# A mixture of experts cut into 28 blocks per layer instead of 31

## The chip, the cores and the metric

The kernel runs on one NeuronCore of a Trainium2 chip. The metric is device time in microseconds (us) for one execution. The engines are PE (TensorE, matrix products; PEld is its weight load), DVE (VectorE), ACT (ScalarE), POOL (GpSimd) and SP (SyncE, which issues the DMAs of the weight stream).

## What is computed

A network of 256 tokens of width 1024: two layers with a mixer (a gated MLP, then block attention) and a mixture of experts, followed by two layers of feed-forward, pooling and recurrence. The change touches the two mixtures of experts. Cut to what matters:

```python
scores = jax.nn.sigmoid(xt @ w_router)            # 256 tokens, 64 experts
choice = where(emask, scores + e_bias, NEG_INF)    # 4 of 8 groups of experts stay
_, eidx = lax.top_k(choice, 8)                     # 8 experts for each token
w = take(scores, eidx); w = w / w.sum(-1) * 2.5
routed = sum over the 8 of w * ((silu(x @ wg[e]) * (x @ wu[e])) @ wd[e])   # width 1024 -> 256 -> 1024
shared = swiglu(xt, ws_gate, ws_up, ws_down)       # one expert for all tokens
return routed + shared
```

All of it is fp32. An expert's three matrices are 3 MB. There are 256 x 8 = 2048 pairs of token and expert, 32 for an expert on average, and the number for each is known only when the router has run.

## The kernel before

All weights come through one stream: SP issues DMAs of 1024 KB, in an order fixed when the program is built, into `ring`, nine slots of 1024 KB. The DMA for a slot waits until the products that read the slot before are done. `pump` issues as far ahead as the ring allows. One slot is one third of an expert: gate and up for the first half of the input features, the same for the second half, and down.

In a mixture of experts (`moe`) the experts are ranked by the number of their tokens, on the chip. The routed experts are computed in blocks of 128 token places each. A block of kind H holds one expert with up to 128 tokens, M two experts with up to 64 each, L four with up to 32 each. `HCAP, MCAP, LCAP` (line 25) give the number of blocks of each kind; the ranks are handed out in that order, so the H blocks take the experts with the most tokens. `blocks_of_ranks` spreads the kinds evenly over the order of work. Tokens beyond a capacity are counted in `route5`, and `overflow` (L1208 to L1237) computes them in a loop over all 64 experts, one at a time, only when there are any.

The order of work on PE is written out by hand, one step for each block b:

- `gu(b, 0)` and `gu(b, 1)`: the gate and up products (L285, read as `ring` and `farena`, output 512 wide), each half needing one slot for each expert of the block; between them `htr(b - 1)`, two transposes (L1156);
- `dn(b - 1)`: the down products of the block before (`ring` and `tmp`), one slot for each expert;
- `pre(b + 1)`: a few small products for the weights and the scatter matrix of the next block (L1120);
- `gather`: half of the gather of the tokens of the next pair of blocks, 16 products of `rarena` with `WH` and `WL` (the tokens);
- `scat(b - 1)`: 16 products that put the block's output back in token order, and four sums on DVE (L1204).

For each expert of a block, `gu` and `dn` use their own columns of the PE array: 128 for H, 64 for each of two in M, 32 for each of four in L, so that the block's experts are side by side in the array. Each `gu` half streams as many slots as there are experts. `htr` of a block needs its activation on ACT and DVE, so it is put behind the first half of the next block's `gu`. In the first five steps the shared expert's products stand among these, and two half slots of its weights (`shd`) in the stream.

Of the kernel before, what the change touches and what calls it, by code (L numbers as in the profile page):

```python
# [24 lines left out]
HCAP, MCAP, LCAP = 12, 12, 7  # L25
# [47 lines left out]
class Item:  # L73
    # slots of the weight stream with whether they are split, matrix products, stages of what follows them,
    # the ring slots that these may take, which buffers of split weights the item still uses otherwise,
    # and how many stages come before the next split
# [7 lines left out]
class Split:  # L84
# [3 lines left out]
    def __call__(self, c, n):  # L88
        # columns c .. c + n of the slot
        b, o = divmod(c, 1024)  # L90
        return self.hi[b][:, o:o + n], self.lo[b][:, o:o + n]
# [3 lines left out]
def moba_moe_hybrid_kernel(ctx: ExitStack, tc: tile.TileContext, A: dict):  # L95
# [14 lines left out]
    x = sb([128, KD, T], F32, "x")  # L110
# [32 lines left out]
    def rview(off, n):  # L143
        # operands in float32r
        assert off + n <= RW, (off, n)
        return rarena[:, off:off + n]
# [11 lines left out]
    # ---------------------------------------------------------------- weight stream  # L158
# [9 lines left out]
    def spare(slot, n, off=0):  # L168
        # fp32 scratch in slots that the stream leaves alone
        v = ring[:, slot:].rearrange("p s f -> p (s f)")  # L170
        return v[:, off:off + n]
# [21 lines left out]
    def ring_slots(*slots):  # L193
        # from here on the stream uses these slots; the others are scratch until it gets them back
        def hold():
            st["held"] = set(range(NRING)) - set(slots)
        add(hold, nsplit=0)
        st["nring"] = slots
# [8 lines left out]
    def run():  # L207
# [14 lines left out]
        def split_halves(idx):  # L222
            # the halves of the next slot to split, if its buffers are free
            q = stt["next"]
            if q >= len(order) or q >= stt["used"] + 2:
                return
            j = order[q]
            n = items[j].first
            if any(idx < i < j and q % 2 in items[i].fence for i in fences) or n >= st["issued"]:
                return  # L230
            stt["next"] += 1
            w = items[j].slots[0][0][2]
            parts = []
            for c in range(0, w, 1024):
                m = min(1024, w - c)
                b = (q % 2) * 2 + c // 1024
                parts.append((WH[:, b, :m], WL[:, b, :m], slot_ap(n)[:, c:c + m]))
            handles[j] = Split([p[0] for p in parts], [p[1] for p in parts])
            for hi, lo, raw in parts:
                S.copy(hi, raw)  # L240
            yield
            for i, (hi, lo, raw) in enumerate(parts):
                V.tensor_sub(lo, raw, hi)  # L243
                if i == len(parts) - 1:
                    donef[n] = True
                    pump()
                yield
# [35 lines left out]
    # ---------------------------------------------------------------- small pieces  # L283
# [31 lines left out]
    def rsqrt_cols(v, y, a, n=2):  # L315
        # v: fp32 columns; y: result
        V.tensor_scalar(a.bitcast(I32), v.bitcast(I32), 1, None, op0=ALU.logical_shift_right)
        V.tensor_scalar(y.bitcast(I32), a.bitcast(I32), -1, 0x5F3759DF, op0=ALU.mult, op1=ALU.add)
        for _ in range(3):
            V.tensor_mul(a, y, y)  # L320
            V.scalar_tensor_tensor(a, a, -0.5, v, op0=ALU.mult, op1=ALU.mult)
            V.scalar_tensor_tensor(y, a, 1.5, y, op0=ALU.add, op1=ALU.mult)
# [3 lines left out]
    def sq_buf():  # L326
        # eight chunks of squares
        return [t[:, i * T:(i + 1) * T] for t in [tmp512() for _ in range(4)] for i in range(2)]
# [4 lines left out]
    def stat_mm(sqs, b=STB):  # L333
        # sums of four chunks at a time, on the four column groups
# [4 lines left out]
    def stat_sum(between=None):  # L339
        # sum over the groups (and 32 equal rows of each) to one column per half of the tokens  # L340
# [23 lines left out]
    def mod_h(Ac, Bc, H, L, ks=range(KD)):  # L364
        # H + L = x * A * R + B, per feature chunk
# [20 lines left out]
    def proj_a(w, p, H, L):  # L386
        # token-major: 256 columns
# [5 lines left out]
    def down_d(w, hid, first, last):  # L393
        # hid: two (H, L) chunks; accumulates all 8 output chunks in banks 0..3
# [17 lines left out]
    # ---------------------------------------------------------------- constants  # L412
# [17 lines left out]
    def lru_consts():  # L430
        # 4 * softplus(-lam); pool bias times pool scale
# [6 lines left out]
        # log1p(e) = 2 atanh(e / (2 + e))  # L438
# [18 lines left out]
    # ---------------------------------------------------------------- ada vectors  # L457
    GB = 6

    def gemv_items(g, out, bname, boff, bank=GB):  # L460
        # eight weight slots; out: [128, 16] columns
# [21 lines left out]
    def gemv_half(h, out, bname, boff, bank=GB):  # L483
        # half as many columns, two rows of the slots at a time; out: [128, 8] columns
# [24 lines left out]
    def interleave(main, side, per):  # L509
        # spread side items among main ones, `per` main items to one side item  # L510
# [28 lines left out]
    # ---------------------------------------------------------------- gMLP (layer 0)  # L539
# [5 lines left out]
    def gmlp():  # L545
# [67 lines left out]
        for s in range(8):  # L613
# [11 lines left out]
            def post2(s=s):  # L625
                # a quarter of the normalised v
# [7 lines left out]
        def spatial(j):  # L634
            # chunks 2 j and 2 j + 1, of group j
# [64 lines left out]
    # ---------------------------------------------------------------- routing: what needs no token, and scores  # L700
# [5 lines left out]
    def route_prep(l):  # L706
        # router rows times the modulation's scale, and what its shift contributes
# [15 lines left out]
    # The weights of the shared expert's first hidden chunk wait where the sum of outputs will be, those of the second wait split.  # L723
# [11 lines left out]
    def shared_second(l):  # L735
        # an item that splits the second hidden chunk's
# [23 lines left out]
    # ---------------------------------------------------------------- swiglu with split weights  # L760
# [10 lines left out]
    def raw_start(lst):  # L771
        # the first three of a list of (arguments of up_pe, post stages, slots): they work on h without the norm's row
        # factor, which comes about meanwhile; their posts follow the third
# [8 lines left out]
    def swiglu_items(uname, u0, dname, d0, nch, hidH, hidL, evac, fin, nh, opts=None, lag=0):  # L782
        # hidden chunks pairwise; evac(p, H, L) of a chunk; fin after the last down slot
# [57 lines left out]
    # ---------------------------------------------------------------- mixture of experts  # L841
# [4 lines left out]
    def moe(l, tail):  # L846
        # the buffers of split weights that come free first hold the tokens, the others the outputs
        # and the weights of the shared expert
# [47 lines left out]
        # ---- norm, router logits  # L896
        def route1():
# [10 lines left out]
            for i in range(4):  # L908
                # token-major copies of x, times the norm's row factor
# [27 lines left out]
        def route1b():  # L937
            p = PB[RB]
            # counts (replicated rows and a column), exact in bfloat16
# [7 lines left out]
            # ranks by descending count  # L947
# [10 lines left out]
        def route2():  # L958
            # positions, weights, order of capacities
# [12 lines left out]
            # into the order of ranks  # L972
# [13 lines left out]
            # for route5  # L986
# [10 lines left out]
        def route5():  # L997
            # capacities by expert, and what goes beyond them
# [19 lines left out]
        # ---- the shared expert, by halves of weight slots among the blocks  # L1018
        sgate = view(6400, T)

        def shw(j):
            if j in (2, 3):
                return SHU1[j - 2]
            # the first output comes later than the second half
# [37 lines left out]
        # ---- blocks of slots  # L1062
# [99 lines left out]
        def dn(b):  # L1162
# [15 lines left out]
            # with the last block the buffers of the tokens become those of split weights again, with scat_last the rest  # L1178
# [111 lines left out]
    # ---------------------------------------------------------------- attention (layer 1)  # L1290
    def attention():
# [9 lines left out]
        # outputs take the place of h  # L1301
# [27 lines left out]
        def kq(nm, s, H, L):  # L1329
# [15 lines left out]
            def hq():  # L1345
                # h of the queries, by pieces
# [14 lines left out]
        def scores(s):  # L1361
            # heads pairwise, masked, softmax over the keys of the upper and the lower half of the queries
# [31 lines left out]
        def weights():  # L1394
            # divide by the sums
# [57 lines left out]
    def att_start(upd):  # L1453
        # residual sums and squares; what the norms of layer 1 scale by
# [13 lines left out]
    # ---------------------------------------------------------------- block 2  # L1468
# [3 lines left out]
    def transition(upd, gname, goff):  # L1472
        # residual sum, the next h (without the norm's row factor) and squares, chunk by chunk
# [14 lines left out]
    # The second block's input is rmsnorm(x) * fin = x R1 fin, whose own norm has the row factor  # L1488
    # R2 = rsqrt(R1^2 mean((x fin)^2) + eps): its first product works on x fin gain, and R1 R2 follows.
# [84 lines left out]
    def hybrid(l, fin):  # L1574
# [131 lines left out]
        def lru_heads(*cs):  # L1706
            # 1 - a^2 = tanh(z / 2) (1 + a)^2 where a = exp(-z)
# [90 lines left out]
        # output chunk m of w_lru_up is complete after unit 10 m + 9  # L1798
# [15 lines left out]
def pack(inp):  # L1814
# [23 lines left out]
    up = lambda w, m: w.reshape(8, 128, -1, m, 128).transpose(2, 1, 3, 0, 4).reshape(-1, 128, 2048)      # (k p) (s m c)  # L1838
    down = lambda w: w.reshape(-1, 2, 128, 1024).transpose(0, 2, 1, 3).reshape(-1, 128, 2048)             # (s kk p) n
    vproj = lambda w: w.reshape(8, 128, -1, 256).transpose(2, 1, 0, 3).reshape(-1, 128, 2048)             # (k p) (s c)  # L1840
    gated = lambda w: w.reshape(8, 128, 2, -1, 128).transpose(3, 1, 2, 0, 4).reshape(-1, 128, 2048)       # (k p) ab (j c)
# [57 lines left out]
```

## Time and profile before

| | |
|---|---|
| median of 3 runs | 2657.63 us (2657.23 to 2666.97) |
| span of the profiled execution | 2661.0 us (its page gives no other time for it) |
| PE busy | 2536.1 us (95%) |
| ACT, DVE busy | 1069.4 us (40%), 1390.8 us (52%) |
| DMA of expert weights | 384 transfers of 1024 KB |
| mean DMA rate over the span | 272 GB/s |
| first expert DMA of layer 0, of layer 1 | 234.4 us, 947.5 us after the start |
| first matmul of the last down product, layer 0, layer 1 | 782.6 us, 1497.6 us |

Matmuls overlap in the array, so a busy PE is not PE at its peak: the order and the starts of its instructions say more than their durations. The rate of the DMAs in a stretch, in GB/s, tells how near the stream is to what it can move; the share of time in which PE waits for it stands in the timeline.

### The profile page before, as it was taken

Reading aid. Unit: us, or ns where it says so; the run is one execution under the profiler, and the core shown is the slowest. Engines: PE = TensorE matmul, PEld = TensorE weight load, DVE = VectorE, ACT = ScalarE, POOL = GpSimd, SP = SyncE. Lnnn points to the kernel's source line nnn. Section 1 sums busy time; section 2 is a strip of 40 time slices with the busy share of each in tenths; the row PEclk is TensorE's granted clock in tenths of the full one; section 3 lists DMA queues with packets and bytes.
Section 4 is the critical chain, followed back from the end, with each engine's and each line's share of the span. In section 5 each row is a group of like instructions: output and inputs, shape, how many; then the busy total and the mean of one; then the engine's idle time right before and its main releaser. Section 6 shows DMA issues by size and latency. Waiting matters only on the chain. (4 is left out here: it accounts for less than half of the span.)

```text
span 2661.0 us, 44584 instructions
## 1 busy us (share of the span) xinstructions
PE 2536.1 (95%) x18198; PEld 1971.5 (74%) x18198; DVE 1390.8 (52%) x2598; ACT 1069.4 (40%) x1766; POOL 3.8 (0%) x6
## 2 busy tenths in 40 slices
PE   6998999999989979999999899999999999999998
PEld 4885554555447845545554599999999999999998
DVE  4555233333347643323333465688655655887655
ACT  3433222222225532222222344576544544685543
POOL 0000000000000000000000000000000000000000
PEclk8999999999999989999999999999999999999999
DMA  9878899999976469999999745354655554454750
GB/s 377 317 269 333 330 374 402 396 404 384 380 293 259 178 279 354 358 422 378 399 404 382 274 167 188 124 188 175 244 183 189 176 189 159 152 178 163 264 188 17
DMA packets 101442, 724.51 MB, mean 272 GB/s; under 512 B 11248, under 2 KB 12528, under 8 KB 14192
## 3 DMA queue, kind: packets, MB, share of 16 engines
q1 hardware_dynamic: 100080, 718.32, 69.1%
q8 instruction: 146, 2.39, 0.4%
q10 hardware_dynamic: 1152, 3.28, 0.3%
q14 instruction: 64, 0.52, 0.1%
HBM read 720.50 MB, written 1.05 MB: 271 GB/s over the span
## 5 line engine op out<-in xcount | busy, mean ns | idle before, releaser
L285 PE MATMUL pb<-rarena,WH 128*128 128x256 f32 x3664 | 722.6, 284 | 36.4 <-DVE farena L1204 23.8
L240 ACT CAST WH<-ring 128x1024 fp32r<-128x1024 f32 x476 | 489.5, 1047 | 454.4 <-PE pb L285 372.5
L285 PE MATMUL pb<-hH,WH 128*128 128x256 f32 x2336 | 665.3, 285 | 3.3 <-ACT hH L1502 2.4
L285 PE MATMUL pb<-hH,WL 128*128 128x256 f32 x2336 | 662.2, 283 | 1.4 <-DVE WL L243 1.4
L285 PE MATMUL pb<-hL,WH 128*128 128x256 f32 x2336 | 661.8, 283 | 0.0
L243 DVE TENSOR_TENSOR WL<-ring,WH 128x1024 fp32r<-128x1024 f32 x476 | 570.9, 1216 | 146.6 <-ACT WH L240 132.8
L285 PEld LDWEIGHTS pb<-rarena,WH 128*128 128x128 f32 x3664 | 598.4, 190 | 54.6 <-ACT farena L1107 33.3
L285 PE MATMUL pb<-rarena,WL 128*128 128x256 f32 x2336 | 616.5, 280 | 3.6 <-DVE WL L243 2.3
L285 PE MATMUL pb<-ring,farena 128*32 128x512 f32 (+2 forms) x2064 | 464.9, 598 | 7.8 <-DMA ring<-ex 7.8
L285 PEld LDWEIGHTS pb<-hH,WH 128*128 128x128 f32 x2336 | 448.9, 192 | 15.6 <-ACT WH L240 5.0
L285 PEld LDWEIGHTS pb<-hH,WL 128*128 128x128 f32 x2336 | 448.8, 192 | 2.0 <-DVE WL L243 1.9
L285 PEld LDWEIGHTS pb<-hL,WH 128*128 128x128 f32 x2336 | 449.0, 192 | 0.2 <-DVE hL L1499 0.2
L285 PEld LDWEIGHTS pb<-rarena,WL 128*128 128x128 f32 x2336 | 444.2, 190 | 5.0 <-DVE WL L243 3.0
L285 PEld LDWEIGHTS pb<-ring,farena 128*32 128x32 f32 (+2 forms) x2064 | 150.8, 135 | 231.2 <-issue 207.5
L285 PE MATMUL pb<-ring,tmp 128*32 128x512 f32 (+2 forms) x1024 | 246.4, 608 | 14.7 <-PEq L1216 5.8
L1144 DVE SCALAR_TENSOR_TENSOR tmp<-pb,small,tmp 128x256 f32<-128x256 f32 x62 | 30.0, 484 | 423.4 <-ACT tmp L1142 423.4
L285 PEld LDWEIGHTS pb<-ring,tmp 128*32 128x32 f32 (+2 forms) x1024 | 78.8, 136 | 176.7 <-issue 157.4
L1177 DVE TENSOR_TENSOR WL<-pb,WH 128x512 fp32r<-128x512 f32 x124 | 85.8, 692 | 193.0 <-ACT WH L1176 193.0
L1204 DVE TENSOR_TENSOR farena<-farena,pb 128x512 f32<-128x512 f32 x232 | 149.1, 684 | 70.6 <-PE pb L285 70.6
L828 DVE TENSOR_TENSOR tmp<-pb,R 128x512 f32<-128x512 f32 x88 | 60.8, 691 | 203.0 <-PE pb L285 199.0
L1107 ACT ACTIVATE farena<-pb,adac,Acol 128x256 f32<-128x256 f32 x256 | 124.9, 561 | 72.0 <-PE pb L285 71.7
L1176 ACT CAST WH<-pb 128x512 fp32r<-128x512 f32 x124 | 72.8, 587 | 199.3 <-PE pb L285 199.3
(302 smaller groups left out, 1644.9 us busy)
## 6 DMA issues: line engine op xcount, KB each, us to landing
ring<-ex SPq DMA_DIRECT2D x384, 1024.0 KB, 12.0
ring<-ada SPq DMA_DIRECT2D x56, 1024.0 KB, 8.1
ring<-f1u SPq DMA_DIRECT2D x44, 1024.0 KB, 4.9
ring<-f2u SPq DMA_DIRECT2D x44, 1024.0 KB, 5.0
ring<-win SPq DMA_DIRECT2D x40, 1024.0 KB, 4.8
ring<-f1d SPq DMA_DIRECT2D x22, 1024.0 KB, 4.8
ring<-f2d SPq DMA_DIRECT2D x22, 1024.0 KB, 4.8
ring<-lu SPq DMA_DIRECT2D x10, 1024.0 KB, 4.7
```

The source lines that it names most:

```text
L240: S.copy(hi, raw)
L243: V.tensor_sub(lo, raw, hi)
L285: P.matmul(out, l, r, start=start, stop=stop, skip_group_check=True, **kw)
L828: V.tensor_tensor(t.rearrange("p (a t) -> p a t", a=2), hold["p"].rearrange("p (a t) -> p a t", a=2), R.rearrange("p (o t) -> p o t", o=1) ...
L1107: S.activation(xg[:, pi % 2, k], bank[:, i * T:(i + 1) * T], AF.Identity, scale=Acol[:, 2, k:k + 1], bias=sh2(l)[:, k:k + 1])
L1144: V.scalar_tensor_tensor(hh, bank[:, 256:], wsl[:, b % 2:b % 2 + 1], t[:, :256], op0=ALU.mult, op1=ALU.mult)
L1176: S.copy(yH[:, fs], PB[DN[f]])
L1177: V.tensor_tensor(yL[:, fs], PB[DN[f]], yH[:, fs], op=ALU.subtract)
L1204: V.tensor_tensor(a2, a2, bank, op=ALU.add)
```

## The change

The counts of blocks of each kind change: two H and three M fewer, two L more. The 64 experts stay (10 + 2 x 9 + 4 x 9, before 12 + 2 x 12 + 4 x 7), and so do the 192 transfers of their weights in each layer, in the same order of use within a block. The capacities by rank become 128 for the first 10, 64 for the next 18 and 32 for the last 36 (before: 12, 24, 28).

```diff
-HCAP, MCAP, LCAP = 12, 12, 7
+HCAP, MCAP, LCAP = 10, 9, 9
```

The rest of the diff only takes out comments. The order of the kinds that `blocks_of_ranks` makes, before and then now:

```
LHMLHMHMLHMLHMHMLHMHMLHMHMLHMHM
LHMLHMLHMLHMLHMLHMLHMLHMLHMH
```

On PE in layer 0, the step of block 6 (`pb_63` and `pb_64` are the PSUM banks of gate and up, `pb_65` and `pb_66` those of down, `farena` the gathered tokens, `tmp` the hidden values, `rarena` with `WH` and `WL` a scatter):

```order
 L285 MATMUL pb_68<-rarena,WH 128x256
 L285 MATMUL pb_68<-rarena,WL 128x256
-L285 MATMUL pb_63<-ring,farena 128x512 x4
+L285 MATMUL pb_63<-ring,farena 32x512 x16
 L1156 MATMUL pb_64<-cst,tmp 128x128 x2
-L285 MATMUL pb_63<-ring,farena 128x512 x4
+L285 MATMUL pb_63<-ring,farena 32x512 x16
 L285 MATMUL pb_65<-ring,tmp 64x512 x2
```

Where an H block stood, with one slot of weights in each half, there is an L block, with four in each half.

On PE at the end of layer 0, the last step with a `gu`; before:

```order
L285 MATMUL pb_63<-ring,farena 64x512 x8
L1156 MATMUL pb_64<-cst,tmp 128x128 x2
L285 MATMUL pb_63<-ring,farena 64x512 x8
L285 MATMUL pb_65<-ring,tmp 128x512
L285 MATMUL pb_66<-ring,tmp 128x512
```

and now:

```order
L285 MATMUL pb_64<-ring,farena 128x512 x4
L1156 MATMUL pb_63<-cst,tmp 128x128 x2
L285 MATMUL pb_64<-ring,farena 128x512 x4
L285 MATMUL pb_65<-ring,tmp 64x512 x2
L285 MATMUL pb_66<-ring,tmp 64x512 x2
```

The last block is an H after an M, where it was an M after an H. Since 28 is even, the last pair of blocks is whole; with 31 it held one block and a half of zeros, and its gather was as long as the others. The instructions of the other stages are the same.

## Rows read from the trace of the kernel before

**Rows 1.** The page: its first line, and the busy time of each engine.
```profile
span 2661.0 us, 44584 instructions
PE 2536.1 (95%) x18198; PEld 1971.5 (74%) x18198; DVE 1390.8 (52%) x2598; ACT 1069.4 (40%) x1766; POOL 3.8 (0%) x6
```

**Rows 2.** Stretches of both expert stages; last columns: granted PE clock, DMA share, GB/s.
```profile
370.00:410.00 40.00, 39.20 (x222) 19.60 (x221) 13.43 (x33) 8.16 (x17) 0.00 (x0) 1.00 0.83 313
410.00:510.00 100.00, 95.45 (x515) 49.18 (x512) 32.21 (x71) 23.22 (x48) 0.00 (x0) 1.00 1.01 420
330.00:750.00 420.00, 405.98 (x2244) 214.38 (x2243) 142.09 (x313) 99.92 (x205) 0.00 (x0) 1.00 0.96 392
1040.00:1460.00 420.00, 407.56 (x2252) 214.44 (x2248) 141.49 (x312) 101.12 (x207) 0.00 (x0) 1.00 0.96 392
```

**Rows 3.** DMAs of expert weights: issues, time to landing, SP's waits for PE.
```profile
ring<-ex SPq DMA_DIRECT2D x384, 1024.0 KB, 12.0
...
DMA to landing us min/median/max: 4.6/12.0/20.1
...
SPq L1074 <- PE pb L285: 518.5, 157, 10.0
```

**Rows 4.** PE timeline, layer 0, 592 to 655: start, busy us, products with weights.
```profile
592.87 3.65 PE L285 MATMUL pb<-ring,tmp 128*64 128x512 f32 x16
...
601.45 3.65 PE L285 MATMUL pb<-ring,farena 128*64 128x512 f32 x16
...
608.99 3.70 PE L285 MATMUL pb<-ring,tmp 128*128 128x512 f32 x8
612.12 0.68 PE L285 MATMUL pb<-rarena 128*128 128x8 f32 x2
...
617.50 3.64 PE L285 MATMUL pb<-ring,farena 128*32 128x512 f32 x32
...
625.01 4.57 PE L285 MATMUL pb<-ring,tmp 128*64 128x512 f32 x16
629.51 0.38 PE L285 MATMUL pb<-rarena 128*128 128x2 f32 x2
...
634.50 3.60 PE L285 MATMUL pb<-ring,farena 128*128 128x512 f32 x8
...
641.68 4.19 PE L285 MATMUL pb<-ring,tmp 128*32 128x512 f32 x32
...
650.88 3.65 PE L285 MATMUL pb<-ring,farena 128*64 128x512 f32 x16
```

**Rows 5.** PE timeline, layer 0: products in which PE waited for weights.
```profile
410.27 4.67 PE L285 MATMUL pb<-ring,tmp 128*64 128x512 f32 x16
...
456.17 1.05 PE L285 MATMUL pb<-ring,farena 128*32 128x512 f32 x4
...
459.98 3.62 PE L285 MATMUL pb<-ring,farena 128*32 128x512 f32 x26 [1.44 <-DMA ring<-ex]
463.53 1.07 PE L285 MATMUL pb<-ring,tmp 128*64 128x512 f32 x2
...
468.54 0.38 PE L285 MATMUL pb<-rarena 128*128 128x2 f32 x2
...
544.40 4.58 PE L285 MATMUL pb<-ring,tmp 128*64 128x512 f32 x16
...
706.24 1.07 PE L285 MATMUL pb<-ring,tmp 128*64 128x512 f32 x2
708.66 3.65 PE L285 MATMUL pb<-ring,tmp 128*64 128x512 f32 x14 [1.35 <-DMA ring<-ex]
```

**Rows 6.** Stretches of 2 us in and after a wait of PE; columns as in rows 2.
```profile
458.00:460.00 2.00, 0.56 (x5) 0.02 (x3) 0.00 (x0) 0.00 (x0) 0.00 (x0) 1.00 1.00 418
782.00:784.00 2.00, 1.35 (x4) 0.59 (x6) 1.44 (x4) 0.00 (x0) 0.00 (x0) 0.50 0.05 8
```

**Rows 7.** PE timeline, end of layer 0: the last down product.
```profile
782.64 6.18 PE L285 MATMUL pb<-ring,tmp 128*64 128x512 f32 x16 [3.26 <-DVE x L1243]
```

## The prediction

> **What bounds the kernel now.** I read the page first: PE is busy for 95% of the span [rows 1]. That is a share of busy time over stages with different limits, so it says only where to look. Next I cut the two expert stages into stretches [rows 2]. In 410 to 510 the stream moves 420 GB/s for 100 us without a break, and in 370 to 410 only 313. Over 420 us of either layer the mean is 392. So the stream runs at its limit in some places and is held up in others, and who holds it up stands in SP's waits: 518.5 us for PE's products to free a slot [rows 3]. The two limits alternate, PE in the stretches with few experts per block and the stream where the blocks of four stand close together. A change that takes work from one of them is therefore worth at most what the other leaves.
>
> Then I read a cycle of blocks in PE's timeline [rows 4]. A block's gate and up products run from 601.45 to 608.99 for an M (7.54 us), from 617.50 to 625.01 for an L (7.51) and from 634.50 to 641.68 for an H (7.18). The reader is to see that these hardly differ: four experts side by side in the array take as long as one, although they read four times the weights. The down product is 3.13 us for an H (608.99 to 612.12). For an M it is 4.50 (625.01 to 629.51), of which 4.57 - 3.65 = 0.92 is a wait for weights (the same product lasts 3.65 at 592.87), so 3.58 in itself; I take the same for an L. PE's time goes by blocks, the stream's by experts, and the change trades the one against the other: fewer blocks, the same 192 transfers.
>
> **What the change saves on PE.** A step from one block's start to the next is 16.05 us (601.45 to 617.50), 17.00 - 0.92 = 16.08 (617.50 to 634.50) and 16.38 - (4.19 - 3.65) = 15.84 (634.50 to 650.88), without waits. Taking the products above from each leaves 5.38, 4.99 and 5.08 us for the rest of a step (small products, gather, scatter), 5.15 in the mean. A block thus costs 7.18 + 3.13 + 5.15 = 15.5 us as H, 16.3 as M, 16.2 as L. The change removes two H and three M and adds two L: 2 x 15.5 + 3 x 16.3 - 2 x 16.2 = 47.5 us for a layer. One more half gather goes, because 31 blocks need as many gathers as 32: about 2 us (5.15 less the small products is two runs of 16 products, 2.2 each at most). Together 49.5 us for a layer, 99 for both, if nothing else ended last. DVE and ACT lose the same steps; they are half busy [rows 1], so their share is counted at nothing. The cover is PE itself, which they follow in each step; without it the four DVE sums of a scatter would be next.
>
> **What the stream gives back.** A transfer is 1024 KB, 1.0486 MB; at 420 GB/s it takes 2.50 us. Seven experts, one L, one H and one M, are 21 transfers or 52.4 us. PE needs 16.05 + 16.08 + 15.84 = 48.0 us for these three blocks. The new order is nine such triples and a last H, so PE must wait 52.4 - 48.0 = 4.4 us in each triple once the ring's stock is used up. Before, the order had HM between the triples more often, and there the stream could catch up.
>
> When is the stock used up? The kernel before shows it. The first six blocks have the same kinds as now. Before, the next L came after LHMHM, and its following down product waited 4.67 - 3.65 = 1.02 us (at 410). The L after that came only three blocks later, and it paid in full: from 456.17 to 468.54 is 12.37 us for half a gate product and a down product that need 3.6 + 3.58, a wait of 5.2 us [rows 5]. That is the new order's steady state, seen once, and near the 4.4 of the sum. So I count one wait of 1.0 us at the third L and 4.4 at each of the six after it: 27.4 us. The waits that stood there before go: 1.02, 5.2, 0.93 (at 544), 0.92 and 3.65 + 708.66 - 706.24 - 3.65 = 2.42 (at 706), 10.5 us. Net 16.9 us a layer, and the gain is 49.5 - 16.9 = 32.6.
>
> The stream alone gives a second way to the same number. In 330 to 750 it could have moved its bytes in 420 x 392 / 420 = 392 us, 28 us less [rows 2]; layer 1 has the same mean. No gain in that stretch can exceed this unless the rate rises. Outside it the stage's end is shorter by an H in place of an M (about 0.8 us of products), and the last stretch of the stream, after 750, has some room too; 28 to 33 us. I take 33 a layer, 66 for both. The profiled span of 2661.0 is 3.4 us above the median of the runs (0.13%), so I subtract from the median: 2657.6 - 66 = **2592 us**; a profiled span would be about 2595.
>
> **Unknown sizes.** The trace shows no expert stage in which the stream is full from the third L to the end. The rate's bounds are 420 GB/s, the highest held for 100 us, and 392, the mean; I take 420, since the 100 us contain the dense passage LHML that the new order repeats. At 406, halfway, a triple is 54.2 us, and six triples lose 6 x 1.8 = 11 us a layer: 2614. A rate above 420 for so long isn't in the rows; 5 GB/s more would give 0.6 us a triple, 7 us in both layers. The wait per triple lies between the 4.4 of the sum and the 5.2 measured; the larger value would take 10 us off the gain of both layers. SP issues the same DMAs; its loads of expert numbers fall by three a layer, and it waits for PE anyway. The transfers of the next stage follow the last expert's on the same queue as before, and both end earlier together.
>
> The Trainium skill, "DMA: Bandwidth & Descriptors", section "Specifications", gives a fabric ceiling of 435 GB/s. The trace holds 420, and the measurement decides; by 435 a triple would be 50.6 us, the net waits some 11 us a layer smaller, and the time an estimated 2570.
>
> **Rivals.** (a) *PE loses its clock in the waits.* In the wait of 458 to 460 PE was busy for 0.56 of 2 us and the granted clock stayed at 1.00, its 2.4 GHz level. After the wait at the end of layer 0, which followed a sparse stretch, it was 0.50, 1.2 GHz [rows 6], and the down product took 6.18 us [rows 7] instead of 3.65, so 2.5 more. One such product a triple hides in the 4.4 us of slack. Three would make a triple 48.0 + 7.5 = 55.5 us, 3.1 more than the stream's, over six triples and two layers 37 us: 2629. The row at 458 speaks against it. The Trainium skill, "TensorE: Matmul & The Clock Gate", section "HAM oscillation", states the mechanism: a loop whose products wait for a DMA at every step can be throttled again at every wait. By that rule the time would be this rival's; the trace has the wait without the drop, once.
>
> (b) *Nine slots are too few.* A block of four takes four slots for half its gate products and frees them all at its end; if the stream then runs dry for a moment in every triple, its mean stays at 392. A triple is then 21 x 1.0486 / 392, 56.2 us, and nine of them lose 34 us a layer: no gain at all, 2657. Halfway is the 2614 above. For it speaks that a transfer alone lands after 4.6 us, so that its slot is empty for longer than its share of the stream; against it that the median is 12.0 us [rows 3], so that several are under way at a time, and that the stream held 420 through the dense passage.
>
> (c) *The stream doesn't bind*, and the whole 99 us come: 2559. It would need 21 transfers in 48.0 us, 459 GB/s. No stretch shows that.
>
> (d) *Slower: tokens go over the capacities.* Then `overflow` loops over all 64 experts with one buffer, three loads each that land after 4.6 us at the earliest: 64 x 3 x 4.6 = 883 us for a layer, over 3500 us in all. It decides from one token on. Ranks 29 to 36 now hold 32 tokens, before 64. Worked out from the reference on its inputs, the largest count is 118 in layer 0 and 121 in layer 1 (capacity 128), the 11th 52 and 53 (64), the 29th 32 and 30 (32). So everything fits, in layer 0 with no place to spare: the 29th and the 30th are both 32. The smallest margin by which a token's eighth choice could become an expert at 32 is 0.009 of a score in layer 0, and the smallest between a token's fourth and fifth group 0.0003, both far above rounding in fp32.
>
> **How the numbers follow.** Forecast, 2570 to 2612: 0.80. (a) with one slow product too many, up to 2635: 0.05. (b) 0.09, of which 0.03 with no gain left. (c) and other ways to under 2570: 0.04. (d) 0.02. The range of 2570 to 2612 takes in the rate's bounds to halfway and the longer wait. A measurement of this kernel can tell about 0.5%, 13 us, from no change: faster 0.95, same 0.03, slower 0.02.
>
> **What would show it.** In the changed profile: a mean rate near 420 over the last 350 us of each expert stage; waits for `ring<-ex` of 4 to 5 us in nearly every triple, half in the second half of the L's gate products, half in the M's down product before it ends; the same 15.5 to 16.3 us of work for a block; SP's waits for PE fewer; the granted clock at 1.00 through the stage; the last down product of layer 0 near 750 us, of layer 1 near 1432. I am wrong if the rate stays near 392, if the clock falls in the waits, or if PE doesn't wait.

## The result, and the profile after

| | before | 28 blocks |
|---|---|---|
| median of 4 runs each | 2658.30 us | 2600.91 us (2598.22 to 2602.33) |
| ratio, 95% interval | | 0.9775 (0.9758 to 0.9792) |
| span of the profiled execution | 2661.0 us | 2596.2 us |

The changed kernel takes 57 us less. The forecast was 2592, 66 us less, with 2570 to 2612 as its range. The two profiled executions differ by 64.8 us. Between two medians it is 57, since the profiled execution of before was on the slow side of its runs and that of after on the fast side: a run's time is 2.0 us above its span here (2598.22 and 2596.2), so a span of 2661.0 stands for about 2663, above the median of 2658.

The page of the changed kernel, where [rows 1] stood:

```profile
span 2596.2 us, 43882 instructions
PE 2457.5 (95%) x17938; PEld 1914.2 (74%) x17938; DVE 1359.0 (52%) x2536; ACT 1041.8 (40%) x1710; POOL 3.8 (0%) x6
```

PE's share is the same 95% as before. Nothing in this row says that the bound has moved. The stretches of the two expert stages say it, against [rows 2] (last columns: granted PE clock, DMA share, GB/s):

```profile
370.00:410.00 40.00, 38.59 (x232) 18.60 (x234) 13.21 (x30) 7.98 (x17) 0.00 (x0) 1.00 0.99 403
410.00:510.00 100.00, 93.83 (x542) 46.55 (x539) 30.56 (x68) 22.95 (x48) 0.00 (x0) 1.00 1.01 421
330.00:710.00 380.00, 358.83 (x2064) 181.59 (x2063) 121.90 (x273) 84.63 (x174) 0.00 (x0) 1.00 1.01 419
1014.00:1394.00 380.00, 359.83 (x2059) 179.93 (x2061) 120.25 (x269) 84.41 (x174) 0.00 (x0) 1.00 1.01 420
```

The stream moved 392 GB/s over such a stretch before. Now it holds 419 and 420 for 380 us in both layers, and 313 has become 403 in the stretch where it had been held up. The time to landing of the expert weights, against [rows 3]:

```profile
DMA to landing us min/median/max: 4.8/12.8/20.8
```

and in the view of SP's waits:

```profile
SPq L1074 <- PE pb L285: 516.2, 164, 10.0
```

SP waits for PE as long as it did (518.5 before), where the prediction had fewer waits: all nine slots are still taken when it comes to the next transfer, whichever side is late. Its long wait for slots, from which the prediction began, doesn't tell which side is the bound. PE's waits for weights, as sums over the span, were before (PEld is the weight load, which waits first):

```profile
PEld pb L285 <- DMA ring<-ex: 32.4, 25, 3.0
...
PE pb L285 <- DMA ring<-ex: 13.5, 12, 2.1
```

and are now:

```profile
PEld pb L285 <- DMA ring<-ex: 65.1, 44, 2.7
...
PE pb L285 <- DMA ring<-ex: 29.2, 34, 1.8
```

These sums double. The timeline shows where, one triple of layer 0 to the next, against [rows 4, 5]:

```profile
421.76 3.64 PE L285 MATMUL pb<-ring,farena 128*32 128x512 f32 x32
425.69 2.21 PE L285 MATMUL pb<-ring,farena 128*32 128x512 f32 x6
429.34 3.62 PE L285 MATMUL pb<-ring,farena 128*32 128x512 f32 x26 [1.44 <-DMA ring<-ex]
432.89 1.07 PE L285 MATMUL pb<-ring,tmp 128*64 128x512 f32 x2
434.31 3.65 PE L285 MATMUL pb<-ring,tmp 128*64 128x512 f32 x14 [0.35 <-DMA ring<-ex]
442.79 3.59 PE L285 MATMUL pb<-ring,farena 128*128 128x512 f32 x8
...
458.53 3.65 PE L285 MATMUL pb<-ring,farena 128*64 128x512 f32 x16
...
474.50 3.64 PE L285 MATMUL pb<-ring,farena 128*32 128x512 f32 x32
...
684.86 3.64 PE L285 MATMUL pb<-ring,farena 128*32 128x512 f32 x32
```

The second half of the L's gate products lasts from 425.69 to 432.89, 7.20 us where 3.57 are needed. The down product behind it begins with two records and goes on 1.42 us later. That is a wait of 5.05 us in this triple. The bracketed waits of PE alone, 1.44 and 0.35, miss most of it: the few products whose slot has landed run by themselves in between, as the two at 432.89 that take 1.07 us, and that counts as busy. From the L at 421.76 to the L at 684.86 are five triples, 52.6 us each; the sum from the stream's rate had 52.4.

### The profile page after: what moved, and what is told of

Its sections match the earlier page's. It is cut to its first block, busy times and chain, and to the rows that moved or that the text cites. A ratio compares the mean times of both kernels' runs of the same rounds, so it can differ in the third digit from the quotient of the medians.

```text
span 2596.2 us, 43882 instructions
## 1 busy us (share of the span) xinstructions
PE 2457.5 (95%) x17938; PEld 1914.2 (74%) x17938; DVE 1359.0 (52%) x2536; ACT 1041.8 (40%) x1710; POOL 3.8 (0%) x6
## 5 line engine op out<-in xcount | busy, mean ns | idle before, releaser
L285 PE MATMUL pb<-rarena,WH 128*128 128x256 f32 x3552 | 691.8, 283 | 34.8 <-DVE farena L1204 22.3
L285 PEld LDWEIGHTS pb<-rarena,WH 128*128 128x128 f32 x3552 | 574.8, 189 | 51.8 <-ACT farena L1107 28.4
L285 PE MATMUL pb<-rarena,WL 128*128 128x256 f32 x2224 | 588.4, 280 | 3.6 <-DVE WL L243 2.3
L285 PE MATMUL pb<-ring,farena 128*32 128x512 f32 (+2 forms) x2064 | 436.0, 595 | 21.4 <-DMA ring<-ex 21.2
L285 PEld LDWEIGHTS pb<-rarena,WL 128*128 128x128 f32 x2224 | 422.2, 190 | 5.7 <-DVE WL L243 3.0
L285 PEld LDWEIGHTS pb<-ring,farena 128*32 128x32 f32 (+2 forms) x2064 | 136.9, 130 | 238.3 <-issue 187.1
L285 PE MATMUL pb<-ring,tmp 128*32 128x512 f32 (+2 forms) x1024 | 228.0, 603 | 16.2 <-PEq L1216 8.2
L285 PEld LDWEIGHTS pb<-ring,tmp 128*32 128x32 f32 (+2 forms) x1024 | 69.3, 131 | 169.5 <-issue 146.1
L1204 DVE TENSOR_TENSOR farena<-farena,pb 128x512 f32<-128x512 f32 x208 | 133.6, 683 | 58.9 <-PE pb L285 58.9
L1158 ACT COPY tmp<-pb 128x256 f32<-128x256 f32 x56 | 20.8, 372 | 287.5 <-PE pb L1156 287.5
```

Source lines behind the costliest of these rows:

```text
L285: P.matmul(out, l, r, start=start, stop=stop, skip_group_check=True, **kw)
L1158: S.copy(t, bank[:, :256])
L1204: V.tensor_tensor(a2, a2, bank, op=ALU.add)
```

## The experiments

The theory: in each moment the later of PE's work and the nine-slot stream sets the pace; the change takes 49.5 us of PE work from a layer and hands back what the stream can't follow. The rivals: PE still ends last and its waits are by the way; or the stream is simply full from end to end; or the count of blocks decides and their order is of no account.

**The stream made lighter, with 28 blocks** (`e1_half_bytes`).

```diff
-                nc.sync.dma_start(slot_ap(nslot), src[...])
+                w = 2048 if l == 0 else 1024
+                nc.sync.dma_start(slot_ap(nslot)[:, :w], src[...][:, :w])
```

> The changed kernel; in layer 1 alone each expert DMA moves only the first half of its slot, so the other half holds old weights and the output of layer 1's routed experts is not the reference's. PE's instructions are the same. Theory (in the new order the weight stream ends last, 52.3 us for each L, H, M against 48 us of PE work): PE's waits for expert weights in layer 1, some 30 us by the timeline, go, and the time falls by 25 to 32 us against the changed kernel, to about 2572. Rival (PE's own work ends last and its waits are by the way): less than 5 us.

Measured: 2566.4 us (ratio to before 0.9644, 0.9619 to 0.9669), 34.5 less than the changed kernel. The changed kernel was not timed again beside the experiments; the kernel before was, at 2660.2 and 2661.3 us instead of 2658.3, so differences to the changed kernel are uncertain by 2 to 3 us. Part of the 34.5 is scatter ahead of and in the untouched layer 0, where the last down product came at 749.06 instead of 753.73. From there to the last one of layer 1 it is 649.5 us against 680.4, so 30.9 us are layer 1's. In the view of waits, the weight loads of layer 1 in the changed kernel, and then with half the bytes, where this is PE's only wait for weights in the layer:

```profile
PEld pb L285 <- DMA ring<-ex: 30.1, 21, 2.3
...
PEld pb L285 <- DMA ring<-ex: 0.8, 1, 0.8
```

and a stretch of its middle:

```profile
1040.00:1360.00 320.00, 311.86 (x1903) 160.40 (x1902) 109.60 (x248) 78.45 (x162) 0.00 (x0) 1.00 0.67 230
```

With 230 GB/s asked of it the stream ends last no more, but for those 0.8 us, and what the views showed as waits, about 30 us in the layer, is all that comes back. The rival that PE ends last falls.

**PE's work made lighter, with 28 blocks** (`e2_less_pe`), and both edits on the kernel before (`e5_half_bytes_before`, `e6_less_pe_before`).

```diff
-                        for j, y in enumerate((yH, yL)):
-                            mm(bank[...], y[:, fs], STm[:, b % 3], j == 0, j == 1)
+                        ys = (yH, yL) if l == 0 else (yH,)
+                        for j, y in enumerate(ys):
+                            mm(bank[...], y[:, fs], STm[:, b % 3], j == 0, j == len(ys) - 1)
```

> The changed kernel; in layer 1 alone the scatter of each block but the last leaves out the low half of the outputs (8 of 16 products, about 0.93 us a block, 25 us for 27 blocks), so the routed sum of layer 1 is rounded more coarsely. The transfers are the same. Theory (stream ends last in the middle of the stage, PE only at its two ends): 5 to 9 us less than the changed kernel, about 2594, and PE's waits for weights in layer 1 grow by some 18 us. Rival (PE ends last): the full 25 us less, about 2576.

> The kernel before with 31 blocks; as in the first experiment only half of each slot is moved in layer 1 (the output of its routed experts is not the reference's). Theory: in the order of 31 blocks the stream ended last only near the blocks of four that stood three apart, about 14 us of waits in the layer, so 12 to 18 us less than the kernel before, some 2644, half or less of what the same edit gave with 28 blocks (34.5). Rival (a fixed price of half transfers, the same in both): 30 us or more.

> The kernel before with 31 blocks; the scatter without the low half in layer 1, as in the second experiment, 30 blocks and 28 us of products. Theory: PE ends last over most of the stage, so 20 to 26 us less than the kernel before, about 2636, against 7 us with 28 blocks. Rival (the stream ended last before too): 10 us or less.

| | 28 blocks | 31 blocks |
|---|---|---|
| half the bytes in layer 1 | 2566.4, 34.5 less (30.9 in the layer) | 2646.5, 14.8 less (ratio 0.9953, 0.9936 to 0.9970) |
| fewer scatter products in layer 1 | 2593.8, 7.1 less (ratio to before 0.9745, 0.9720 to 0.9770) | 2643.5, 17.8 less (ratio 0.9935, 0.9918 to 0.9952) |

One number was mis-sized, for 31 blocks: 20 to 26 expected, 17.8 measured. And the second row can't be compared with the first as it stands, because lighter scatters shorten the very end of the layer too. With 28 blocks, from the first H block's gate product to the end of layer 1, the changed kernel:

```profile
957.93 3.59 PE L285 MATMUL pb<-ring,farena 128*128 128x512 f32 x8
...
1422.19 3.65 PE L285 MATMUL pb<-ring,tmp 128*64 128x512 f32 x16
...
1434.17 6.64 PE L285 MATMUL pb<-ring,tmp 128*128 128x512 f32 x8 [4.68 <-PEq L1216]
```

and with the lighter scatter:

```profile
956.09 3.59 PE L285 MATMUL pb<-ring,farena 128*128 128x512 f32 x8
...
1420.01 3.65 PE L285 MATMUL pb<-ring,tmp 128*64 128x512 f32 x16
1427.80 5.37 PE L285 MATMUL pb<-ring,tmp 128*128 128x512 f32 x8 [0.73 <-DVEq L1217]
```

With 31 blocks, the kernel before (its last down product is at 1497.60) and then with the lighter scatter:

```profile
991.02 3.59 PE L285 MATMUL pb<-ring,farena 128*128 128x512 f32 x8
...
1484.51 3.70 PE L285 MATMUL pb<-ring,tmp 128*128 128x512 f32 x8
...
986.51 3.59 PE L285 MATMUL pb<-ring,farena 128*128 128x512 f32 x8
...
1470.56 3.70 PE L285 MATMUL pb<-ring,tmp 128*128 128x512 f32 x8
...
1478.36 5.35 PE L285 MATMUL pb<-ring,tmp 128*64 128x512 f32 x16 [0.72 <-DVEq L1217]
```

From the last down product but one to the last it takes 7.8 us in both kernels with lighter scatters, against 12.0 and 13.1 (12.1 and 13.3 with half the bytes): PE waits 0.7 us at the test for overflow (L1216, in the edited file L1217) instead of 4.7 and 5.8. Why is not shown. That is neither limit of the stage, and it makes up 4.2 of the 7.1 us and 5.3 of the 17.8. The stage up to there shows the bound (with half the bytes it runs from 953.17 to 1386.51 and from 985.88 to 1466.31):

| layer 1, first H block to the last down product but one | 28 blocks | 31 blocks |
|---|---|---|
| unchanged | 464.3 | 493.5 |
| half the bytes | 433.3, 30.9 less | 480.4, 13.1 less |
| fewer scatter products | 463.9, 0.3 less | 484.1, 9.4 less |

With 28 blocks lighter PE work is worth almost nothing there, with 31 blocks 9.4 us against the lighter stream's 13.1. The bound has moved: it was mixed, and is now the stream's but for the two ends of the stage. The edit also frees less PE time than its products took. With 31 blocks a step from an M's first gate product to the next block's is 15.50 us (1225.37 to 1240.87), against 15.97 for the same step of layer 1 before (1234.47 to 1250.44), so 0.47 instead of 0.93. PE now waits 0.64 us for ACT's evictions of the gather at this place, where it had waited 0.42 for DVE's sum:

```profile
1224.43 1.01 PE L285 MATMUL pb<-rarena,WH 128*128 128x256 f32 x4 [0.64 <-ACT farena L1107]
1225.37 3.65 PE L285 MATMUL pb<-ring,farena 128*64 128x512 f32 x16
...
1240.87 3.64 PE L285 MATMUL pb<-ring,farena 128*32 128x512 f32 x32
```

With 0.47 a step, the 29 steps of the stage give 13.6 us with 31 blocks, of which 9.4 came through, and the 26 with 28 blocks give 12.2, of which 0.3 did. There the weight loads take up what PE was spared: they wait 37.0 us in layer 1 instead of 30.1, 7 us more, where 18 were expected. A triple still takes 52.2 us, as this timeline of the second edit shows in layer 1, and 52.5 in the mean of five (1097.34 to 1359.85), against 52.6 in the changed kernel (1100.75 to 1363.92):

```profile
1097.34 3.64 PE L285 MATMUL pb<-ring,farena 128*32 128x512 f32 x32
...
1149.53 3.64 PE L285 MATMUL pb<-ring,farena 128*32 128x512 f32 x32
...
1157.81 5.32 PE L285 MATMUL pb<-ring,farena 128*32 128x512 f32 x26 [1.44 <-DMA ring<-ex]
```

**One block fewer again** (`e3_27_blocks`).

```diff
-HCAP, MCAP, LCAP = 10, 9, 9
+HCAP, MCAP, LCAP = 8, 10, 9
```

> Capacities 8, 10, 9: one block fewer in each layer (two H fewer, one M more), all counts of tokens still fit (9th largest 54 and 56, 29th 32 and 30). The PE work falls by 2 x 15.5 - 16.3 + about 1 = 15 to 16 us a layer. Theory: the stream is full in the middle already, but it still idles at the start, where the shared expert's products hold PE; the order begins L, M, L and uses some of that: 8 to 11 us less a layer, 2579 to 2585. Rival (PE ends last): 31 us less, 2570. A stream that is full throughout: no gain, 2601.

Measured: 2583.7 us (ratio to before 0.9703, 0.9675 to 0.9731), 17.3 less than with 28. That is neither the 31 of PE's work nor nothing: the stream still had idle time at the start of a layer, and the order that begins L, M, L uses some of it. The start of layer 0 in the change, and then in this run, 388 GB/s where the change has 321:

```profile
270.00:330.00 60.00, 57.14 (x356) 33.74 (x355) 12.96 (x30) 15.30 (x32) 0.00 (x0) 0.98 0.84 321
...
270.00:330.00 60.00, 56.73 (x367) 32.48 (x369) 11.78 (x27) 14.36 (x30) 0.00 (x0) 0.97 0.95 388
```

**The same 28 blocks in another order** (`e4_order28`), the 31 blocks in an order without waits (`e12_order31`), and 28 sorted by kind (`e8_sorted`).

```diff
+    kinds = list("LHLHLMMHLHMMLMMHLHHLHMMMLHHL")
     nxt = {"H": 0, "M": HCAP, "L": HCAP + 2 * MCAP}
```

> The 28 blocks of the change in another order, LHLHLMMHLHMMLMMHLHHLHMMMLHHL: more blocks of four at the start, where the stream idled, and one at the end; the same instructions and bytes. Theory (at each moment the later of PE and the stream with its nine slots): PE's waits fall from about 30 to 11 to 15 us a layer, 16 to 19 us less a layer, 2563 to 2570. Rival (the change's gain is the smaller count of blocks and its order is of no account): within 5 us of 2601.

> The kernel before with its 31 blocks (12, 12, 7) in an order that leaves PE no waits by the sum: HLMHLHHLHMMHLHMMHLHHLHMMMMMMMHL. Theory: only the 14 us of waits a layer can go, 2630 to 2634; PE's own work then ends last, and no order of 31 blocks reaches the 28. Rival (the order is what counts, not the number of blocks): near 2601 or below.

> The 28 blocks of the change in the order ten H, nine M, nine L: the same instructions and bytes, full computation. Theory: the nine slots cannot carry the stream's spare time of the H and M blocks over to the L blocks, each L then costs 12 transfers or 30 us where PE needs 16, PE waits about 111 us a layer instead of 30, and the time is 2755 to 2770, slower than with 31 blocks. Rival (the number of blocks decides): near 2601.

Measured: 2570.2 us (ratio to before 0.9655, 0.9630 to 0.9680) for the reordered 28, 30.7 less than the change; 2630.4 (0.9888, 0.9872 to 0.9905) for the reordered 31; 2764.3 in a single run for the sorted 28, 101 more than a single run of the kernel before beside it (2662.9). The reordered 28 at the start of layer 0, and in the middle:

```profile
270.00:330.00 60.00, 58.90 (x384) 37.47 (x383) 14.71 (x35) 16.23 (x33) 0.00 (x0) 0.98 0.90 364
330.00:710.00 380.00, 365.42 (x2090) 189.02 (x2089) 125.20 (x275) 88.99 (x183) 0.00 (x0) 1.00 1.01 417
```

Again the first stretch is above the change's 321 GB/s. The extra blocks of four at the start take weights while PE has the shared expert to do. The 43 GB/s more are 2.6 MB in these 60 us, 6 us of the stream at 420 GB/s, an estimate from these rows; the last down product of layer 0 came 16.4 us earlier (737.37). The sum also counts a gain from the L at the end, after which PE has less left to work off; no run shows that part alone. The sorted order shows the opposite:

```profile
280.00:430.00 150.00, 146.03 (x671) 91.16 (x671) 51.02 (x106) 39.53 (x80) 0.00 (x0) 1.00 0.56 200
430.00:580.00 150.00, 145.04 (x814) 71.47 (x812) 48.94 (x109) 35.34 (x73) 0.00 (x0) 1.00 0.96 384
580.00:830.00 250.00, 191.49 (x1083) 68.45 (x1078) 49.87 (x118) 30.72 (x63) 0.00 (x0) 0.91 1.01 421
```

200 GB/s among the H, 384 among the M, 421 among the L. Nine slots did not carry the bandwidth that the H and M left over to the L. In the reordered 31 these are all of PE's waits for weights, in the whole span:

```profile
who waited for it (us, times):
  PEld pb L286: 0.8, 2
```

So the rival of the count falls: the number of blocks decides nothing by itself, since 28 blocks can be slower than 31. But the order of 31 alone doesn't reach the 28 either: it has no wait for weights left to lose, PE's own work ends last, and it is at 2630.

**Both together** (`e7_order27`): 8, 10, 9 and the order LMLHLMMHLHMMLHHLMHLHMMLHMML.

> 27 blocks (8, 10, 9) in the order LMLHLMMHLHMMLHHLMHLHMMLHMML, the two improvements together, full computation. Theory: at each moment the later of PE and the nine slots; 22 to 26 us less a layer than the changed kernel, 2549 to 2557. If the two gains simply added (17 and 31): 2553. Rival (the stream is already full in the reordered 28): no gain over its 2570.

Measured: 2555.6 us (ratio to before 0.9601, 0.9585 to 0.9617), 45 less than the change and the fastest of the kernels here. Its stream in the same two places:

```profile
270.00:330.00 60.00, 57.67 (x376) 32.62 (x376) 12.63 (x29) 15.24 (x31) 0.00 (x0) 0.98 0.95 388
330.00:700.00 370.00, 355.52 (x2045) 183.79 (x2043) 122.24 (x272) 85.47 (x176) 0.00 (x0) 1.00 1.01 418
```

**Tokens over the capacity** (`e11_over`).

```diff
-HCAP, MCAP, LCAP = 10, 9, 9
+HCAP, MCAP, LCAP = 10, 7, 10
```

> 27 blocks as 10 H, 7 M, 10 L, so that ranks 25 to 64 hold 32 tokens: the 25th has 36 in layer 0 and 35 in layer 1, some tokens go over, and the loop over all 64 experts runs in both layers. Full computation. Rival (d) of the prediction priced it at 64 x 3 x 4.6 = 883 us a layer at the least, so 4350 us or more; with the products of each expert behind its loads in one buffer, up to 8000. If the loop cost little after all, the time would be near that of the other 27 blocks, 2584.

Measured: 10006.7 us in a single run, above the 8000 that I had as the most. The DMA issues of the loop, in the view of DMAs:

```profile
farena<-ex SPq DMA_DIRECT2D x384, 1024.0 KB, 4.8
```

and SP's timeline in it:

```profile
2018.10 21.83 SPq L1225 DMA_DIRECT2D farena<-ex  x2
2060.63 0.33 SPq L1235 DMA_DIRECT2D farena<-ex  x1
2076.03 21.87 SPq L1225 DMA_DIRECT2D farena<-ex  x2
```

One expert takes 57.9 us (2018.10 to 2076.03); 128 of them are 7415, and 10006.7 - 2583.7 (the other 27 blocks) is 7423. The prediction's 883 us a layer were the landings alone. The products cost more: with one buffer each load waits for those that read it before, so the third of an expert goes out 42.5 us after the first (2018.10 and 2060.63).

## Why the prediction was right

- *PE's time goes by blocks, the stream's by experts.* Right; the L, H and M of the new timeline last what they did, and with half the bytes PE's work stood alone and was no longer than the sum had it: a triple took 47.9 us (1093.16 to 1141.05) where the sum had 48.0, and the layer was shorter by the waits of the timeline.
- *49.5 us of PE work saved in a layer.* By layer 0 it holds. Its last down product came 28.9 us earlier, the stage began 0.5 later, so it gained 29.4. The waits added come to about 19 (next point), together 48.5.
- *Net waits of 16.9 us.* This is the term that was too small. For the L at 421.76 and the five after it the wait, read as above, is 4.2 to 5.8 us, 28.2 in all, where six times 4.4 made 26.4. At the third L it is 1.2 in the M's down product and 1.4 in the L's own, where 1.0 stood for both. That is 30.8. The old waits were more than the 10.5 that the prediction took off: it left out two in an L's down product, 0.64 (the product at 427.05 took 4.29 us) and the 0.54 that it takes out of a step itself, so they are 11.7 and the net is 19.1. Of the 4.2 to 5.8 us only 1.4 stand in the M's down product and the rest in the L's gate products; the prediction had half in each. Per triple the wait was 4.8 in the five measured, 0.4 more than the sum: half of it is the triple (52.6 against 52.4), half PE's work (47.8 against the 48.0 of one cycle).
- *28 us from the stream alone.* This was the better of the two ways, and I took 33, the top of its 28 to 33. Measured for layer 0: 29.4. Layer 1 gained 33.6 from its first expert DMA (947.46 and 917.63) to its last down product (1497.60 and 1434.17), but 3.3 of that lies ahead of the first H block, where the first gate products took 5.4 and 5.3 us before and 4.5 and 3.6 after, at different granted clocks (0.88 in 963 to 977 before, 1.00 in 934 to 944 after). Without these the two layers gained 29.4 and 30.3 us where 33 each were forecast.
- *A profiled span of about 2595.* It came at 2596.2, and that is luck: the 3.3 us just named and the distance of both profiled executions from their medians made up for the waits that were too small. Between the medians the forecast missed by 9 us.
- *The range.* It claims to take in the halfway rate, but the prediction's own sum for that, 2614, lies 2 us outside it. The measured time lies well inside either.
- *The stream holds 420.* Right, for 380 us at a stretch.
- *The ends.* The last down products were forecast near 750 and 1432; they came here:

```profile
753.73 5.37 PE L285 MATMUL pb<-ring,tmp 128*128 128x512 f32 x8 [3.47 <-PEq L1216]
```

and at 1434.17, as shown above.

The rivals: (a) didn't occur in the change, in spite of waits in every triple from the fourth L on. In one of them PE was busy for a third of the time and kept 1.00, the level of 2.4 GHz; this row answers to [rows 6]:

```profile
428.00:430.00 2.00, 0.66 (x8) 0.29 (x12) 0.00 (x0) 0.00 (x0) 0.00 (x0) 1.00 1.00 418
```

The loop of the Trainium skill's "TensorE: Matmul & The Clock Gate", section "HAM oscillation", falls to the lower clock at every wait for a DMA. In the change the trace has such waits without the fall, but with products in between and no wait of PE for weights over 1.8 us, so it is not that loop; in the sorted order the clock fell in some of them (below). (b) and (c) are excluded by the rate; (d) by the time, though its price was too low by a factor of four.

## What to carry to other kernels

Where work is packed to use one engine better, price a unit on each resource apart: here a block costs PE the same whether it reads 3 MB or 12, and the saving ends where the stream is full. Then look at the order before cutting further: with the same blocks it was worth 31 us one way and 163 the other, as I read it because a ring of nine slots evens out only what lies a few blocks apart; no run had another number of slots. A fixed capacity that the inputs just fill (32 of 32) is fast until one token more costs 58 us for each of 64 experts of its layer.

## What the runs showed of the hardware

The lower clock of TensorE came back where waits were more frequent. In the sorted order's blocks of four, layer 0:

```profile
724.00:728.00 4.00, 2.41 (x4) 0.14 (x2) 0.00 (x0) 0.00 (x0) 0.00 (x0) 0.82 1.02 426
728.00:732.00 4.00, 3.29 (x16) 0.79 (x20) 0.00 (x0) 0.00 (x0) 0.00 (x0) 0.50 1.02 426
```

The granted clock was 0.50, 1.2 GHz, after a stretch in which two products at a time alternated with waits of about 1.4 us; in the 12 us before that stretch, with waits alike, it was still 1.00. With the scatter made lighter it fell twice: the products at 1157.81 and 1263.69 took 5.32 us instead of 3.62. It cost little or nothing there, since the weights ended last: the triples with them took 52.5 and 52.6 us, the other three of the five 52.0 to 53.2.
